# The dt product of the first queries: a score buffer as its target instead of the projections' bank

## The chip, the cores and the metric

The kernel runs on one core of a Trainium2 chip. The metric is the time of one execution on the device in microseconds (us). TensorE is called PE here, ScalarE ACT, VectorE DVE, GpSimd POOL and SyncE SP; PSUM is the memory of eight banks into which PE writes its products.

## The reference, cut to what matters

Two layers over 1024 latent tokens and 256 context tokens of width 1024: attention first, then a Mamba-2 style scan (SSD). Each layer norms its input, shifts and scales it, and adds its gated result back.

```python
h, hc = x, ctx
for i in range(DEPTH):                      # DEPTH = 2
    u = rms_normalize(h) * (1.0 + scale[:, None]) + shift[:, None]
    uc = rms_normalize(hc) * (1.0 + scale_c) + shift_c
    if i % N_MIXERS == 0:
        y, yc = attention_mixer(u, uc, ...)
    else:
        y, yc = ssd_mixer(u, uc, ...)
    h = h + gate[:, None] * y
    ...
# in ssd_mixer, for the context and for the latent tokens
z, xbc, dt_raw = jnp.split(h @ w_in, [SSD_WIDTH, SSD_WIDTH + SSD_CONV_DIM], axis=-1)
xbc = silu(centred_depthwise_conv(xbc, conv_w, conv_b))
dt = softplus(dt_raw.reshape(...) + dt_bias_dir)
```

`dt_raw` is a product of the normed input with 64 columns of the input weights. From `dt` come the decays of the scan, which all heads need.

## The kernel before, in words

Tokens are held in three blocks: block 0 (latent 0 to 511), block 1 (latent 512 to 1023) and block 2 (the 256 context tokens). The normed and modulated input of each block stands in two parts, `uH` and `uL`, a rounded value and its rest, and so does each weight (`wh`, `wl`); a product is three matmuls for each of the eight slices of the width (lines 238 to 240, in `mm3`).

Attention's PSUM holds two score buffers `S` of two banks each, one bank `pj` for projections, two `pt` and one `pv`. A call of `t(pool, ...)` takes the next buffer of its name, and the first instruction that writes it waits until the last reader of its former content is done.

At the end of `attention` the last block (block 1) has its output product made for eight column groups, m = 0 to 7; those with m % 3 other than 0 use a score buffer, the others `pj`. Each is read by a gate on DVE (line 840), squared on ACT (847) and summed on DVE (848, `sqa`). Then `dt_setup` has loaded the weights of dt (`wdth`, `wdtl`), and a loop makes two dt products, of block 2 (256 columns) and of block 0 (512 columns), each read by four ACT instructions in `dt_raw` (line 1013, into `cacc`). Last comes `steps[-1]()`: the norm of block 1 and its modulation. The norm sums the squares across partitions on PE (line 361, into `pt`), takes the root on ACT and POOL (369, 370), spreads it by a diagonal (DVE 376, PE 378), and copies the result on ACT (380); the modulation writes `uH1` and `uL1` (299 to 301).

Behind it the scan's layer opens other PSUM pools (`psD`, `psX`, `pj2`) in the same banks. `front` makes the input products of group 0, tile by tile: bT (which becomes B), two tiles of x, cT. For each tile there is a product of the context (line 1179, into `psD`) and one of the latent tokens (1194, into `pj2`), then taps of the convolution on ACT (1093) and DVE (1097), a silu (ACT 1108, DVE 1106), and PE transposes (1148) with ACT copies (1149). In among the first tile stands the third dt product, that of block 1 (line 1204, into `psX`), and when it is read the chain of dt begins (lines 1061 to 1081, mostly DVE), with PE transposes at 1050. Each tile's weights are cast on ACT (1123) and split on DVE (1127). The states of the scan (1297 on PE, 1309 on DVE, `hb`) follow.

The order of all this on each engine isn't written by hand alone. The program is laid out ahead of time by a scheduler with a timeline of its own, which places an instruction where, by that timeline, its engine and data are free. Each engine then works its list off in order.

Of the kernel before, what the change touches and what calls it, by code (L numbers as in the profile page):

```python
# [42 lines left out]
    pj=1, S=2, pt=2, pv=1,  # L43
# [70 lines left out]
class Kernel:  # L114
# [684 lines left out]
    def attention(self, c0, ckv):  # L799
        nc, t, a = self.nc, self.t, self.a  # L800
        ps = self.psA
# [109 lines left out]
        for x, (i, j, b) in enumerate(units):  # L911
            if oH[i] is None:
                if i == 1:
                    i = 0
                    tick(True)
                    i = 1
                    cq.close()
                    self.po = self.pool("op", ctx=c0)
                n = TT[i][1]
# [12 lines left out]
        with ExitStack() as c1:  # L932
            self.o1 = self.pool("o1", ctx=c1, side="right")
            steps = out_steps(1)
            for f in steps[:-1]:
                for _ in f():
                    pass
            self.dt_setup()
            for i, lo in ((2, 256), (0, 0)):
                n = TT[i][1] // 2  # L940
                self.dt_raw(self.dts[:, lo : lo + n], self.proj(ps, self.wdt, i), n)
            for _ in steps[-1]():
                pass
        BUFS.update(wr=2, wh=2, wl=2)
# [852 lines left out]
```

## Time and profile before

| | us |
|---|---|
| median of 3 runs (lowest, highest) | 1774.34 (1774.31, 1775.89) |
| the profiled execution | 1774.14 |
| its span, first to last instruction | 1772.0 |
| PE busy | 1726.3 (97%) |
| DVE busy | 1204.1 (68%) |
| ACT busy | 872.3 (49%) |
| POOL busy | 795.5 (45%) |
| mean granted clock of TensorE | 0.997 |

In the views, a timeline row gives the start, the duration, the engine, the line, the operation, what it writes from what it reads, the count, and in brackets how long the engine was idle before it and what ended that. Matmuls overlap: one of 512 columns has a duration of 0.39 us and follows the one before after 0.23. A row of the chain gives start, time on the chain, engine, tile and line. A row of the waits gives the sum, the count and the longest. A row of stretches gives the span, PE's busy time and instructions, the granted clock of TensorE, the DMA share and GB/s.

### The profile page before, as it was taken

The page shows a single profiled execution, that of the slowest core. Times are in us where ns is not written, and L with a number is a line of the kernel's source. Part 1 is how long each engine was busy: PE and PEld are TensorE (multiplying, and loading weights), DVE is VectorE, ACT ScalarE, POOL GpSimd, SP SyncE. Part 2 cuts the span into 40 slices and gives each one's busy share as a digit, 9 for nine tenths or more (in the row PEclk, how much of TensorE's full clock was granted, in tenths as well). Part 3 has the DMA queues.
Part 4 walks back from the last instruction along what each step waited for, and adds up shares of the span by engine and source line. Part 5 has one row for each costly group of instructions (what it writes and reads, how often), then busy time and mean ns, then how long its engine had stood idle before and what let it go on. Part 6 is the DMA issues. An engine that isn't in the chain of part 4 may idle for free.

```text
span 1772.0 us, 28996 instructions
## 1 busy us (share of the span) xinstructions
PE 1726.3 (97%) x10327; PEld 1492.7 (84%) x10327; DVE 1204.1 (68%) x2121; ACT 872.3 (49%) x1902; POOL 795.5 (45%) x1066
## 2 busy tenths in 40 slices
PE   6999999999999999999999999999999999999997
PEld 4897788888888887778898998989889898988887
DVE  5744447788877775694876867677686767866634
ACT  4522247777787774452544434344444434544522
POOL 3231037555575545104454554636355363554321
PEclk9999999999999999999999999999999999999999
DMA  9568856444464536231323232322333333556533
GB/s 356 174 204 272 294 140 149 101 102 106 115 159 125 131 105 212 72 76 56 76 79 98 72 93 69 87 78 75 90 81 83 81 84 81 183 162 168 183 100 119
DMA packets 211355, 225.51 MB, mean 127 GB/s; under 512 B 15756, under 2 KB 149004, under 8 KB 211212
## 3 DMA queue, kind: packets, MB, share of 16 engines
q1 hardware_dynamic: 177148, 205.02, 39.0%
q0 software_dynamic: 34064, 18.65, 5.7%
q8 instruction: 81, 1.33, 0.3%
q14 instruction: 62, 0.51, 0.1%
HBM read 188.78 MB, written 35.13 MB: 126 GB/s over the span
## 4 chain that ended last, share of the span: by engine, by line
PE 84%; DVE 7%; issue 3%; DMA 2%; ACT 2%; POOL 1%; SPq 0%; DVEq 0%; POOLq 0%; ACTq 0%
PE pj L1194 19%; PE pj L1228 10%; PE pj L1629 7%; PE pj L238 6%; PE pj L240 6%; PE pj L239 6%; PE psD L1179 4%; PE pt L774 3%; PE psX L1381 3%; PE psD L1297 2%; PE pv L781 2%; PE pv L780 2%; PE psX L1350 2%; PE psX L1349 2%; PE S L749 2%
## 5 line engine op out<-in xcount | busy, mean ns | idle before, releaser
L238 PE MATMUL pj<-uH,wh 128*128 128x512 f32 (+1 forms) x680 | 243.8, 359 | 1.3 <-ACT uH L796 0.4
L240 PE MATMUL pj<-uH,wl 128*128 128x512 f32 (+1 forms) x680 | 229.8, 339 | 1.4 <-POOL wl L223 1.4
L239 PE MATMUL pj<-uL,wh 128*128 128x512 f32 (+1 forms) x680 | 230.0, 338 | 0.4 <-POOL uL L797 0.4
L1194 PE MATMUL pj<-uH,wh 128*128 128x512 f32 x512 | 173.4, 410 | 1.2 <-ACT bn L1149 1.2
L1194 PE MATMUL pj<-uH,wl 128*128 128x512 f32 x512 | 170.3, 403 | 0.0
L1194 PE MATMUL pj<-uL,wh 128*128 128x512 f32 x512 | 168.3, 402 | 0.0
L1272 POOL TENSOR_TENSOR xw<-xn,dtdec 128x256 f32<-128x256 f32 x144 | 95.9, 667 | 160.0 <-PE psD L1297 76.0
L1228 PE MATMUL pj<-wh,uH 128*128 128x256 f32 x512 | 150.8, 295 | 0.0
L238 PEld LDWEIGHTS pj<-uH,wh 128*128 128x128 f32 x680 | 129.0, 190 | 25.5 <-ACT wh L221 5.6
L1228 PE MATMUL pj<-wl,uH 128*128 128x256 f32 x512 | 150.2, 293 | 0.0
L1228 PE MATMUL pj<-wh,uL 128*128 128x256 f32 x512 | 149.5, 292 | 0.0
L779 DVE TENSOR_TENSOR pl<-pt,ph 128x512 fp32r<-128x512 f32 x168 | 114.2, 688 | 48.0 <-ACT ph L778 46.8
L240 PEld LDWEIGHTS pj<-uH,wl 128*128 128x128 f32 x680 | 128.7, 190 | 17.5 <-POOL wl L223 2.3
L239 PEld LDWEIGHTS pj<-uL,wh 128*128 128x128 f32 x680 | 129.4, 190 | 10.7 <-issue 1.1
L223 POOL TENSOR_TENSOR wl<-wr,wh 128x512 fp32r<-128x512 f32 x74 | 96.8, 1310 | 87.8 <-ACT wh L221 87.0
L753 DVE CUSTOM_DVE_ANT_0 sm<-S,mask,nsink 128x640 f32<-128x640 f32 (+2 forms) x160 | 119.4, 772 | 21.2 <-PE S L749 15.6
L1413 ACT ACTIVATE uT<-psX,nw 128x128 f32<-128x128 f32 x128 | 46.6, 364 | 170.9 <-PE psX L1412 169.8
L755 ACT ACTIVATE sm<-sm,nm 128x640 f32<-128x640 f32 (+2 forms) x160 | 118.6, 743 | 15.3 <-DVE nm L753 14.7
L778 ACT CAST ph<-pt 128x512 fp32r<-128x512 f32 x168 | 97.6, 586 | 53.4 <-PE pt L774 49.1
L221 ACT CAST wh<-wr 128x512 fp32r<-128x512 f32 (+1 forms) x116 | 74.7, 648 | 82.1 <-PE pj L239 60.3
L1194 PEld LDWEIGHTS pj<-uH,wl 128*128 128x128 f32 x512 | 95.8, 188 | 19.9
L1194 PEld LDWEIGHTS pj<-uL,wh 128*128 128x128 f32 x512 | 95.3, 188 | 19.3
(354 smaller groups left out, 4918.1 us busy)
## 6 DMA issues: line engine op xcount, KB each, us to landing
wr<-w_x SPq DMA_DIRECT2D x32, 512.0 KB, 4.2
M<-acs SPq DMA_DIRECT2D x64, 256.0 KB, 5.1
bw<-acs SPq DMA_DIRECT2D x64, 256.0 KB, 5.5
wr<-w_sk SPq DMA_DIRECT2D x24, 512.0 KB, 4.1
wr<-wg SPq DMA_DIRECT2D x40, 256.0 KB, 4.8
qs<-q POOLq DMA_DIRECT2D x40, 256.0 KB, 3.9
wada<-w_ada SPq DMA_DIRECT2D x16, 512.0 KB, 6.5
wr<-wq SPq DMA_DIRECT2D x32, 256.0 KB, 3.1
```

The source lines that it names most:

```text
L223: (eng or nc.vector).tensor_tensor(l, raw, h, op=ALU.subtract)
L238: self.nc.tensor.matmul(ps, lh, rh, start=first and i == 0, stop=False)
L239: self.nc.tensor.matmul(ps, lh, rl, start=False, stop=False)
L240: self.last_mm = self.nc.tensor.matmul(ps, ll, rh, start=False, stop=last and i == n - 1)
L753: nc.vector.tensor_tensor_reduce(out=sm[:, :W], in0=Sv, in1=self.mask[:, m0 : m0 + W], scale=-SCALE, scalar=self.nsink[:, 4 * j + r : 4 * ...
L755: nc.scalar.activation(sm[:, :W], sm[:, :W], AF.Exp, bias=nm[:, r : r + 1], scale=-1.0, accum_out=sums[:, r : r + 1])
L778: nc.scalar.copy(ph, ptf)
L779: nc.vector.tensor_sub(pl, ptf, ph)
L1194: self.pe = nc.tensor.matmul(raw[:, 512 * i : 512 * i + 512], l[:, k, :], r[i][:, k, :], start=k + y == 0, stop=k == KT - 1 and y == 2)
L1228: self.pe = nc.tensor.matmul(pj[:, c], l, r[:, k, :], start=c % 2 + q + k + y == 0, stop=c % 2 == 1 and q == 1 and k == 3 and y == 2)
L1272: nc.gpsimd.tensor_tensor(xw, X(st, c).rearrange("p (r h) -> p r h", r=R), self.dtdec[:, c, hd(d, g)].unsqueeze(2).broadcast_to([P, R, HP] ...
L1629: self.pe = nc.tensor.matmul(banks[x], l[:, z, sl], r, start=k == 2 * qs[0] and y == 0, stop=k == 2 * qs[-1] + 1 and y == 2)
```

## The change

The product of block 0 is written into a score buffer (`psS`, two buffers of two banks) and no more into `pj`. The product of block 2 stays in `pj`. No product, reading or transfer is added or dropped.

```diff
             for i, lo in ((2, 256), (0, 0)):
                 n = TT[i][1] // 2
-                self.dt_raw(self.dts[:, lo : lo + n], self.proj(ps, self.wdt, i), n)
+                self.dt_raw(self.dts[:, lo : lo + n], self.proj(ps, self.wdt, i, "pj" if i else "S"), n)
```

The scheduler's timeline comes out differently from this place on, until the first slots of the scan, and with it the order on PE, ACT, DVE and (one row) POOL. SP's list stays as it was.

On PE, at the end of attention: `S_8569` is the last output group, `pj_8612` the dt product of block 2, number 8641 that of block 0, `pt_8670` the norm's sum and `pt_8680` its spreading.

```order
 L239 MATMUL S_8569<-uL_1372_5690,wh_8557 128x512
+L238 MATMUL S_8641<-uH_2036_8183,wdth_8601 128x512
 L240 MATMUL S_8569<-uH_1371_5689,wl_8559 128x512
...
 L240 MATMUL pj_8612<-uH_1656_6760,wdtl_8603 128x256
+L239 MATMUL S_8641<-uL_2037_8184,wdth_8601 128x512
...
 L361 MATMUL pt_8670<-ones_68,sqa_8289 128x1 x4
-L238 MATMUL pj_8641<-uH_2036_8183,wdth_8601 128x512
...
 L378 MATMUL pt_8680<-dg_2131_8678,ones_68 128x512
```

The product of block 0 moved ahead of the norm's sum, one of its 24 matmuls into the last output group, and the sum and its spreading now follow each other. Further on PE, eight matmuls of line 1194 that stood ahead of the end of the third dt product (1204) stand behind it; the two transposes (1148) of the first x tile's context product follow directly on the eight of bT; and the eight transposes of that x tile stand behind 24 matmuls of line 1194 and nine of line 1179.

On ACT, at the same place (`rc` is the norm's root, `wh_8833` the cast of the third dt product's weights):

```order
 L1013 ACTIVATE cacc_8611<-pj_8612,db_8605 32x128 x4
+L1123 CAST wh_8833<-wr_8783 128x1024
+L1013 ACTIVATE cacc_8611<-S_8641,db_8605 32x256 x4
 L369 ACTIVATE rc_8675<-pt_8670,eps_70 128x4
-L1123 CAST wh_8833<-wr_8783 128x1024
-L1013 ACTIVATE cacc_8611<-pj_8641,db_8605 32x256 x4
 L380 COPY sqa_8682<-pt_8680 128x512
```

The reading of block 0's product moved ahead of the norm's first step.

On DVE, in the first tiles of the scan's layer: before, from the reciprocal of the dt chain on (`cctx_9009` and `cacc_8926` belong to the first x tile, `wl_9116` is the second x tile's weight).

```order
L1066 RECIPROCAL sz_8885<-sz_8884 128x640
L1106 SCALAR_TENSOR_TENSOR bT_8812<-pj_2172_8811,bT_8812 128x1024
L1097 SCALAR_TENSOR_TENSOR cctx_9009<-psD_8964,cw_8735,cctx_9009 128x254
L1067 TENSOR_TENSOR xn_2178_8883<-xn_2178_8883,sz_8885 128x640
L1127 TENSOR_TENSOR wl_9116<-wr_9061,wh_9114 128x1024
```

And now, the last twelve rows up to the silu of that context product:

```order
L1069 SCALAR_TENSOR_TENSOR cacc_8611<-cacc_8611,xn_2178_8883 128x640
L1097 SCALAR_TENSOR_TENSOR cctx_9009<-psD_8964,cw_8735,cctx_9009 128x255
L1127 TENSOR_TENSOR wl_9116<-wr_9061,wh_9114 128x1024
L1097 SCALAR_TENSOR_TENSOR cacc_8926<-pj_2187_8925,cw_8735,cacc_8926 128x1022
L1070 TENSOR_SCALAR sz_8884<-cacc_8611 128x640
L1071 TENSOR_SCALAR xn_2178_8883<-cacc_8611,al_8607 128x640
L1097 SCALAR_TENSOR_TENSOR cctx_9009<-psD_8964,cw_8735,cctx_9009 128x254
L1106 SCALAR_TENSOR_TENSOR bT_8812<-pj_2172_8811,bT_8812 128x1024
L1097 SCALAR_TENSOR_TENSOR cacc_8926<-pj_2187_8925,cw_8735,cacc_8926 128x1023
L1072 SCALAR_TENSOR_TENSOR sz_8885<-cT_8767,xn_2178_8883 64x640
L1073 SCALAR_TENSOR_TENSOR sz_8885<-cT_8767,xn_2178_8883 64x640
L1106 SCALAR_TENSOR_TENSOR cctx_9009<-psD_8964,cctx_9009 128x256
```

The end of bT's silu (the row L1106 of bT) stood directly behind the reciprocal; now the dt steps 1067 to 1071, the four taps of cctx, the split of the next weight and a tap of cacc stand between them. Two dt steps (1063, 1064) moved the other way, ahead of the split that opens this stretch.

## The prediction

> **What bounds the kernel now.** I read the page's head and its chain first, then who waited for whom on TensorE (PE) between 700 and 870 us, the stretch in which attention hands over to the scan, then the timelines of each engine there, and last the chain in order of time.
>
> ```profile
> span 1772.0 us, 28996 instructions
> PE 84%; DVE 7%; issue 3%; DMA 2%; ACT 2%; POOL 1%; SPq 0%; DVEq 0%; POOLq 0%; ACTq 0%
> ```
>
> PE carries 84% of the chain that ended last. The rows of PE's timeline follow its program's order, with no gap over most of the span, so a microsecond that PE waits is a microsecond of the end, unless a later PE wait becomes shorter by it. The profiled execution took 1774.14 us, its span 1772.0; the median of the three runs is 1774.34, 0.2 above it.
>
> Two waits concern the changed product directly: PE's timeline shows both, each for the reading of the one bank `pj` by ScalarE (ACT).
>
> ```profile
> 719.30 0.28 PE L238 MATMUL pj<-uH,wdth 128*128 128x256 f32 x1
> 722.10 0.95 PE L361 MATMUL pt<-ones,sqa 128*128 128x1 f32 x8
> 724.16 0.50 PE L238 MATMUL pj<-uH,wdth 128*128 128x512 f32 x1 [1.11 <-ACT cacc L1013]
> 729.85 1.02 PE L378 MATMUL pt<-dg,ones 128*128 128x512 f32 x2
> 732.00 0.38 PE L1179 MATMUL psD<-uH,wh 128*128 128x256 f32 x1 [1.13 <-ACT cacc L1013]
> ```
>
> The context's dt product ends at 722.10; the first queries' product may begin only when ACT has emptied the bank (1.11 us lost); the scan's first product (L1179) waits for the second emptying (1.13 lost). Between them stand the norm's sum (L361) and, behind the second product, its spreading (L378), for which nothing was waited.
>
> **The change part by part.** *The two waits (removed).* With a score buffer as its target the second product needs no emptying of `pj`, and the scan's first product finds `pj` read long before. That is 1.11 + 1.13 = 2.24 us of PE waits. Against that, one matmul of the product is now placed inside the last output block's product, where it needs the score buffer's last reader, the gate of block 5:
>
> ```profile
> 713.53 0.74 DVE L840 SCALAR_TENSOR_TENSOR h1k<-S,mod,h1k 128x512 f32<-128x512 f32 x1
> 714.04 0.39 PE L239 MATMUL S<-uL,wh 128*128 128x512 f32 x1
> ```
>
> That reader ends at 714.27, the moment at which PE gets there (714.04 plus one spacing of 0.23). I take 0.1 us, between 0 and 0.3.
>
> *The norm's chain (a new wait).* L361 now stands behind the second product instead of ahead of it, and on ACT the first step of the norm (L369) stands behind the reading of the score buffer. L378 follows L361 directly on PE, so nothing covers the chain in between any more. Its steps:
>
> ```profile
> 722.63 1.47 ACT L1013 ACTIVATE cacc<-pj,db 32x128 f32<-32x128 f32 x4
> 724.13 0.26 ACT L369 ACTIVATE rc<-pt,eps 128x4 f32<-128x4 f32 x1
> 730.05 1.90 ACT L1013 ACTIVATE cacc<-pj,db 32x256 f32<-32x256 f32 x4 [4.72 <-PE pj L240]
> 724.48 1.02 POOL L370 TENSOR_TENSOR rc<-rc,half 128x4 f32<-128x4 f32 x1 [7.41 <-ACT rc L369]
> 726.50 0.68 DVE L376 TENSOR_TENSOR dg<-ident,rc 128x512 f32<-128x512 f32 x1
> ```
>
> PE: 719.30 + 0.23 (the early matmul) + 0.1 + 2.80 (the context's product, 722.10 - 719.30) = 722.4; 23 matmuls of 0.23 (5.7 us from 724.16 to 729.85 for 24) bring 727.8; the last one's tail, 0.39 - 0.23, gives 727.95. Then 1.90 (L1013) + 0.26 (L369) + 0.1 lag + 1.02 (GpSimd) + 0.05 + 0.68 (VectorE) = 4.0: L378 begins near 732.0 and L1179 some 0.85 later, at 732.85, where it was 732.00. PE idles 3.4 us between L361 and L378. So this place alone ends **0.85 us later**, the 2.24 included.
>
> *The order on VectorE (moved, and the largest term).* The order is made ahead of time by a scheduler, and behind the handover it comes out otherwise. On VectorE (DVE) the taps of bT (L1097, L1106) are now mixed with the dt chain and with the next tile's taps, and PE's transposes of bT (L1148) still stand where they stood.
>
> ```profile
> 750.21 1.91 ACT L1013 ACTIVATE cacc<-psX,db 32x256 f32<-32x256 f32 x4
> 752.13 1.06 ACT L1123 CAST wh<-wr 128x1024 fp32r<-128x1024 f32 x1
> 754.58 0.75 ACT L1062 ACTIVATE xn<-xn 128x640 f32<-128x640 f32 x1
> 752.14 0.82 DVE L1061 SCALAR_TENSOR_TENSOR xn<-cacc 128x640 f32<-128x640 f32 x1 [0.58 <-ACT cacc L1013]
> 753.22 1.23 DVE L1127 TENSOR_TENSOR wl<-wr,wh 128x1024 fp32r<-128x1024 f32 x1 [0.25 <-ACT wh L1123]
> 766.04 1.09 PE L1148 MATMUL pj<-ident,bT 128*128 128x128 f32 x8 [0.52 <-DVE bT L1106]
> 768.30 0.74 PE L1194 MATMUL pj<-uH,wh 128*128 128x512 f32 x2 [1.16 <-ACT bn L1149]
> ```
>
> Before, PE reaches the transposes at 765.5 and waits 0.52 us for L1106 of bT; 1.16 us more for the copy behind them. After, PE reaches them 0.85 later, at 766.4. For DVE: the third dt product (L1204) has eight L1194 matmuls fewer ahead of it (8 x 0.23 = 1.8), so ACT's reading of it ends 1.8 - 0.85 = 0.95 earlier, at 751.15; L1061 (0.82), L1062 (0.75) and only then the cast L1123 (1.06) bring 753.8, and the split L1127 begins at 753.85, 0.6 later than its 753.22. Two dt steps (L1063, L1064, 0.40 each) are now done ahead of it. These steps come in between it and L1106 of bT, by the chain's rows:
>
> ```profile
> 757.33 0.40 DVE sz L1064
> 766.37 0.73 DVE xn L1067
> 767.11 1.13 DVE wl L1127
> 768.24 0.39 DVE cctx L1097
> 768.63 1.19 DVE cacc L1097
> 772.14 0.73 DVE cacc L1069
> 774.45 0.40 DVE sz L1070
> 774.85 0.46 DVE xn L1071
> 775.32 0.33 DVE cctx L1106
> 776.84 1.39 DVE sz L1072
> 778.26 1.50 DVE sz L1073
> ```
>
> L1067, L1068 and L1069 at 0.73 each, four taps of cctx at 0.39, the split L1127 1.13, one tap of cacc 1.19, L1070 0.40, L1071 0.46: 6.93 us. L1106 of bT ends 0.6 - 0.80 + 6.93 = 6.7 us later, at 772.75. PE waits 6.35 us there instead of 0.52.
>
> *The next transposes.* Those of the context tile (cctx) now follow at once on PE. Their data come after one tap of cacc, L1072, L1073 and L1106 of cctx: 1.19 + 1.39 + 1.50 + 0.33 = 4.4 us behind L1106 of bT, at 777.15, while PE ends the eight transposes at 773.85: 3.3 us idle. With 0.2 for the two transposes PE begins L1194 of the next tile at 777.35 where it began at 768.30: 9.05 later, of which 0.2 is work done ahead.
>
> *What gets shorter behind that.*
>
> ```profile
> PE pj L1148 <- DVE cacc L1106: 1.4, 1, 1.4
> PE psD L1297 <- DVE hb L1309: 1.2, 2, 0.6
> ...
> 831.86 0.45 PE psD L1297 x2
> 832.88 0.71 PE psD L1297 x2
> ```
>
> Late PE work finds DVE further on: the wait of 1.4 for cacc goes (those transposes now stand behind 33 matmuls, 24 x 0.23 + 9 x 0.12 = 6.6 us, and DVE needs two taps, L1106 and some small dt steps, about 5 us). The state products (L1297) move forward by one place each, so that the bunch at the end, where a pair takes 0.71 instead of 0.45 and the waits sum to 1.2, shrinks: between 1.2 and 2.5 us, I take 2.0. Sum without the clock: 9.05 - 0.2 - 1.4 - 2.0 = **5.45 us**.
>
> *The clock.* The only idle stretch of over 1.4 us in this trace that has work behind it stands at the start:
>
> ```profile
> 24.13 0.80 PE L516 MATMUL pj<-uH,wh 128*128 128x512 f32 x1 [2.79 <-ACT uH L540]
> ...
> 22.00:26.00 4.00, 1.87 (x4) 0.72 1.05 402
> 26.00:30.00 4.00, 4.00 (x24) 0.85 0.90 345
> ```
>
> The granted clock (third figure from the right) falls to 0.72 and 0.85 in those two stretches of 4 us: 4 x 0.28 + 4 x 0.15 = 1.7 us of PE's work lost once, behind an idle time of 2.79. Idle times of 1.1 to 1.4 us show no such loss. The new ones, 3.4, 6.35 and 3.3 us, are all longer; the last two lie a microsecond apart and count as one, and the first is interrupted by L361. I take one loss of 1.6, between 0 and two of them. [...]
>
> Sum: 5.45 + 1.6 = 7.05; 1774.14 + 7.05 = 1781.2 for a profiled execution, 1781.4 beside the median.
>
> **The rivals.** *No loss of clock.* The same waits, PE at full speed behind them: 1774.34 + 5.45 = 1779.8. For it: only one place in the trace shows the loss. Within the forecast's sign. *Two losses*: the wait at L378 has one too, 1774.34 + 5.45 + 3.2 = 1783.0.
>
> *Faster: the freed bank decides.* If bT's taps do not hold PE, because DVE has the reordered steps done by the time PE comes, the handover's 2.24 us of waits, the 1.16 behind the transposes and the 1.4 for cacc are gone with the 2.0 of the state products, and the chain at L378 eats the handover's gain: 1774.34 - 1.16 - 1.4 - 2.0 + 0.85 = 1770.6. It decides if L1106 of bT ends less than 0.5 us behind PE's arrival; by the sums above it is 6.35 behind. Against it: the steps ahead of it are on one engine in a fixed order and their durations are measured. Only a misread order could turn it.
>
> *No difference.* PE loses at the handover but the scan gives most of it back, since its other waits shrink as well. From the list of waits between 700 and 870 us no more than the 1.2 to 2.5 us already counted is there to be given back in this stretch, and later stages of the chain are PE end to end. It would take 3.5 us more than that: 1779.8 - 3.5 = 1776.3.
>
> *The change does nothing there*, if the score buffer shares the wait: the product's 1.11 would stay. It has another reader, gone by 714.27.
>
> **How the numbers follow.** A measurement of this kernel can tell some 0.2%, 3.5 us, from no change: slower is above 1777.9, faster below 1770.8. The forecast with one loss of clock has 0.5, none 0.2, two 0.15: together 0.85, all slower. No difference 0.09, faster 0.06. Bounds: with no loss and 2.5 us given back, 5.45 - 0.5 = 4.95 us, 1779.3; two losses and only 1.2 given back, 5.45 + 0.8 + 3.2 = 9.45 us, 1783.8. I widen the low end by 1.3 for the four durations on DVE that other work could shorten, and leave out the two cases of 0.15: 1778.0 to 1784.0.
>
> **What would show it.** In the profile after: no wait of L238 and L1179 for L1013; a PE wait of 3 to 4 us at L378 for the norm's diagonal (L376); 6 to 7 us at L1148 for L1106 of bT; 3 to 4 us at the transposes of cctx; none at L1148 for L1106 of cacc; granted clock below 1 in one or two stretches near 770 to 785; every stage behind 870 us equally long, only later by 5 to 9. It is wrong if PE's wait for bT is below 3 us, if DVE's steps from that split L1127 to L1106 of bT take much less than 19 us (753.85 to 772.75), or if the shift at 870 us is gone by the end.

## The result, and the profile after

The changed kernel takes 1784.57 us (median of six runs), the kernel before beside it 1775.12: **slower by the ratio 1.0056 (95% interval 1.0039 to 1.0074)**, some 9.9 us. In a second comparison it was 1784.32 to 1775.02, ratio 1.0054 (1.0041 to 1.0066). The forecast was 1781.4 in a range of 1778.0 to 1784.0: the direction held, the size was 3 us short, just past the range's upper end.

The list of waits of TensorE (PE) in the changed kernel, 700 to 885 us (total, times, longest):

```profile
PE pj L1148 <- DVE bT L1106: 6.2, 1, 6.2
PE pt L378 <- DVE dg L376: 3.4, 1, 3.4
PE psD L1148 <- DVE cctx L1106: 2.6, 1, 2.6
```

That is all of it: both waits for the reading of `pj` (L1013) are gone, and so are those for `bn`, `cacc` and `hb`. Three long ones stand in their place. PE's timeline at the three, and the first rows behind:

```profile
729.36 0.95 PE L361 MATMUL pt<-ones,sqa 128*128 128x1 f32 x8
733.72 2.04 PE L378 MATMUL pt<-dg,ones 128*128 128x512 f32 x2 [3.41 <-DVE dg L376]
...
775.85 1.97 PE L1148 MATMUL pj<-ident,bT 128*128 128x128 f32 x8 [6.21 <-DVE bT L1106]
780.41 0.69 PE L1148 MATMUL psD<-ident,cctx 128*128 128x128 f32 x2 [2.59 <-DVE cctx L1106]
780.75 1.20 PE L1194 MATMUL pj<-uH,wh 128*128 128x512 f32 x2
```

Behind each wait the work itself is slow: L378 takes 2.04 us where it took 1.02, bT's eight transposes 1.97 where they took 1.09. The view of stretches says why. The stretches here are cut at the moments where the granted clock changes (span, PE busy, instructions, granted clock, DMA share, GB/s):

```profile
733.63:737.05 3.42, 3.33 (x9) 0.50 0.02 5
...
771.18:774.59 3.41, 0.00 (x0) 1.00 0.37 108
774.59:778.00 3.41, 1.97 (x8) 0.50 0.11 46
778.00:781.42 3.42, 1.01 (x4) 0.50 0.07 18
781.42:784.83 3.41, 3.41 (x10) 0.50 0.24 69
784.83:788.24 3.41, 3.41 (x17) 1.00 0.65 94
```

The clock is at half for one piece of 3.41 us behind the wait at L378, and for three such pieces around the two sets of transposes. What that costs: 3.33 us of PE work at half speed lose 1.67 us; bT's transposes lose nothing, since they end 2.59 us ahead of the next ones' data; from 780.41 to 784.83 PE works at half speed and loses 4.42 / 2 = 2.21. Together **3.9 us**, where the forecast had 1.6.

The profiled execution took 1784.48 us, 10.3 more than that of before. Not all of it belongs to the change: the clock was also low for a moment ahead of the changed place, 0.83 in this stretch of 10 us, where the profile of before has 1.00.

```profile
690.00:700.00 10.00, 8.49 (x29) 0.83 0.55 175
```

Two matmuls that both kernels make give the change's share. One is the first of the context's dt product, at 719.30 in the profile of before (the prediction shows its row). The other stands behind the changed part; here it is in the profile of before, and then both in that of the changed kernel.

```profile
850.54 0.48 PE L1194 MATMUL pj<-uH,wh 128*128 128x512 f32 x1
```

```profile
721.20 0.28 PE L238 MATMUL pj<-uH,wdth 128*128 128x256 f32 x1
...
861.36 0.48 PE L1194 MATMUL pj<-uH,wh 128*128 128x512 f32 x1
```

The first starts 1.9 us later than before, the second 10.8: 8.9 us arise in between. Of these, 3.9 are clock by the sum above, which leaves 5.0 for the waits and the order.

### The profile page after: what moved, and what is told of

Same layout as the page of the kernel before. It is cut to its first block, busy times and chain, and to the rows that moved or that the text cites. A ratio compares the mean times of both kernels' runs of the same rounds, so it can differ in the third digit from the quotient of the medians.

```text
span 1782.4 us, 28994 instructions
## 1 busy us (share of the span) xinstructions
PE 1731.0 (97%) x10327; PEld 1498.0 (84%) x10327; DVE 1204.7 (68%) x2121; ACT 872.7 (49%) x1902; POOL 794.8 (45%) x1066
## 4 chain that ended last, share of the span: by engine, by line
PE 58%; DVE 2%; issue 1%; POOL 0%; ACT 0%; DVEq 0%; POOLq 0%; ACTq 0%
PE pj L1194 19%; PE pj L1228 10%; PE pj L1629 7%; PE psD L1179 4%; PE psX L1381 3%; PE psD L1297 2%; PE psX L1350 2%; PE psX L1349 2%; PE psX L1356 1%; PE pj L240 1%; PE pj L238 1%; PE pj L239 1%; PE psX L1412 1%; PE psX L1347 1%; PE pj L1148 1%
```

## The experiments

In seven of these ten kernels the order was held by a table of instruction numbers for each engine, from the end of attention to the first slots of the scan, from which edges are made that bind the order alone. Three kernels have matmuls added, which shifts line numbers there by up to 15: L1163 is L1148 here, L1117 is L1106, and L281 are the added ones. Times are medians; behind each stands the ratio to the kernel before on the same chip.

| kernel | us | before | ratio (95% interval) |
|---|---|---|---|
| bank alone, order of before | 1771.74 | 1775.29 | 0.9980 (0.9971 to 0.9989) |
| scan's order alone | 1779.17 | 1775.29 | 1.0019 (1.0010 to 1.0029) |
| handover's order alone | 1777.83 | 1775.29 | 1.0018 (1.0009 to 1.0027) |
| changed kernel, stretches filled | 1780.57 | 1775.29 | 1.0026 (1.0016 to 1.0037) |
| sum first | 1772.34 | 1775.21 | 0.9982 (0.9973 to 0.9991) |
| context's product in the score buffer | 1785.55 | 1775.21 | 1.0056 (1.0043 to 1.0069) |
| handover's order, filled | 1776.17 | 1775.21 | 1.0007 (0.9999 to 1.0016) |
| changed kernel, last stretch filled | 1781.73 | 1775.21 | 1.0032 (1.0020 to 1.0044) |
| silu's product early | 1788.56 | 1775.02 | 1.0071 (1.0058 to 1.0085) |
| changed kernel again | 1784.32 | 1775.02 | 1.0054 (1.0041 to 1.0066) |

**The bank alone.** The new bank, with every engine's order as before.

```diff
+def keep_order(tc):
+    at = {i.name: i for i in tc.nc.cur_bb.bb.instructions}
+    for row in ORDER.values():
+        row = [n for n in row if f"I-{n}" in at]
+        for x, y in zip(row, row[1:]):
...
     k.build()
+    keep_order(tc)
```

> The score buffer as the dt product's target, with every instruction on PE, DVE, ACT and POOL in the order of the kernel before. Theory (the changed order costs, the bank itself gains): both waits for L1013 (1.11 and 1.13 us) go, no wait of 3.4 us at L378 and none of 6 us at L1148 appears, no drop of the granted clock between 730 and 790 us; the kernel ends 1.5 to 2.8 us ahead of the kernel before, near 1772.9. Rival (the bank itself costs, by a reader or a transfer that the list of waits doesn't show): most of the 9.9 us stays, at least 5 us slower than before.

It is 3.6 us faster than before (0.0020 of 1775; the interval gives 2.0 to 5.1), a little more than the theory's 1.5 to 2.8, which the interval overlaps. Its waits between 700 and 885 us, without a small one behind them, are those of before less the two for L1013:

```profile
PE pj L1148 <- DVE cacc L1106: 1.4, 1, 1.4
PE psD L1297 <- DVE hb L1309: 1.2, 2, 0.6
PE pj L1194 <- ACT bn L1149: 1.2, 1, 1.2
PE pj L1148 <- DVE bT L1106: 0.5, 1, 0.5
```

So the edit that the diff shows is a gain. What loses is the order that the scheduler makes around it.

**The scan's order alone, and the handover's order alone.** The same edit with another table: up to the norm's spreading (L378) one kernel's order, behind it the other's. Against the table of the bank alone, a piece of DVE's row for the scan's order (8950 is L1106 of bT), and of PE's for the handover's (8642 is the dt product's matmul that slipped into the last output block):

```diff
-8943, 8919, 8950, 9012, 8933, 9117, 9013, 9067, 8940, 9014, 9068, 8947
+8943, 8947, 9014, 9117, 9067, 8954, 8960, 9015, 8950, 9068, 8971, 8991
```

```diff
-8571, 8572, 8573, 8574, 8575
+8571, 8642, 8572, 8573, 8574
```

> The score buffer as target; PE up to the norm's spreading (L378) and ACT up to its copy (L380) in the order of the kernel before, all behind that in the order of the changed kernel. Theory: no wait of 3.4 us at L378 and no drop of the clock there; the wait for bT at L1148 (6.2) and the one for cctx (2.6) stay, with a clock at half for some 10 us around them, of which 2 to 2.5 us cost time: 4 to 5.5 us slower than before, near 1779.5. Rival (the two places aren't independent: the lateness from the handover makes the scan's order costly): the wait for bT shrinks below 4 us, and the kernel is within 2 us of the kernel before.

> The score buffer as target; the handover (PE up to L378, ACT up to L380) in the order of the changed kernel, all behind that in the order of the kernel before. Theory: the wait of 3.4 us at L378 stays, one window of 3.4 us at half clock stands behind it, the waits at L1148 are those of before (0.5 and 1.4): waits 1 us and clock 1.5 us, 2 to 3.5 us slower than before, near 1777.7. Rival (no loss of clock behind 3.4 us of idle time; the stretch at half clock that the changed kernel shows there was chance): 0.5 to 1.2 us slower than before.

The scan's order alone: 3.4 us slower than before by the ratio (3.9 by the medians), just under what was expected, with the waits of 6.3 and 2.6. Its clock:

```profile
769.64:773.05 3.41, 1.97 (x8) 0.50 0.16 65
773.05:776.47 3.42, 1.12 (x4) 0.50 0.07 19
776.47:779.88 3.41, 3.41 (x9) 0.50 0.31 81
779.88:783.29 3.41, 3.41 (x16) 1.00 0.38 88
```

The handover's order alone: 3.2 us slower (2.5 by the medians). The wait of 3.4 us at L378 shows in the first row, one piece of half clock behind it in the second:

```profile
730.28:733.69 3.41, 0.23 (x1) 1.00 0.23 95
733.69:737.10 3.41, 3.41 (x12) 0.50 0.02 5
```

Both rivals fall, and the two places add. Against the bank alone (-3.6) the scan's order costs 3.4 + 3.6 = 7.0, the handover's 3.2 + 3.6 = 6.8, together 13.8; the changed kernel stands 9.8 + 3.6 = 13.4 above it. Each of these differences is known to some 2 us.

**The clock by itself.** The changed kernel's order, with matmuls that nobody reads in the three idle stretches.

```diff
+    def warm(self, pool, tag, size, n):
+        if n:
+            out = pool.tile([P, size], F32, tag=tag, name=f"warm_{tag}_{n}", bufs=BUFS.get(tag, 1))
+            for _ in range(n):
+                self.nc.tensor.matmul(out[:, :512], self.uH[0][:, 0, :P], self.uH[0][:, 0, :], start=True, stop=True)
...
+        if self.warming == 1:
+            self.warm(self.psS, "S", 1024, 14)
...
+                if g == 0 and d is st["bn"][0]:
+                    self.warm(ps, "psX", 512, 27)
+                if g == 0 and d is st["xn"][2] and o == 0:
+                    self.warm(ps, "psX", 512, 12)
```

> The changed kernel in its own order, with matmuls of 128x512 whose product nobody reads put on PE into its three idle stretches: 14 ahead of L378, 27 ahead of the transposes of bT, 12 ahead of those of cctx, 0.23 us each. They take no time that PE would not have waited. Theory (part of the time is TensorE's clock, which drops behind the idle stretches): the granted clock stays at 1 between 730 and 790 us, and the kernel ends 3 to 4 us ahead of the changed kernel, 5.5 to 7 us behind the kernel before, near 1781. Rival (the drops of the clock lie beside waits and cost nothing; the waits and something else make up the 9.9 us): same time as the changed kernel, 9 to 10.5 us behind the kernel before, near 1784.5.

PE's timeline (the added matmuls and the work behind them), then the stretches:

```profile
728.81 3.43 PE L281 MATMUL warm_S<-uH 128*128 128x512 f32 x14
732.36 1.10 PE L387 MATMUL pt<-dg,ones 128*128 128x512 f32 x2
...
766.55 6.28 PE L281 MATMUL warm_psX<-uH 128*128 128x512 f32 x27
772.92 1.09 PE L1163 MATMUL pj<-ident,bT 128*128 128x128 f32 x8
```

```profile
730.00:740.00 10.00, 9.88 (x53) 1.00 0.03 11
760.00:776.00 16.00, 15.91 (x80) 1.00 0.12 33
776.00:786.00 10.00, 9.31 (x55) 1.00 0.34 72
```

More work, and less time: 1780.57, 3.9 us ahead of the changed kernel by the medians (1784.4 as the mean of its two), 5.1 by the ratios (1.0055 less 1.0026). The order on DVE, ACT and POOL is that of the changed kernel, and on PE it differs by the 53 added matmuls alone. The two matmuls of above stand at 719.84 and 856.36 us in this profile: 5.3 us arise between them, 3.6 fewer than in the changed kernel's. What differs is that the clock stays up: the mean granted clock of this kernel's seven executions is 0.994 to 0.998, that of the changed kernel's eleven 0.988 to 0.994, that of the kernel before 0.992 to 0.997. So the rival falls: those 3.6 to 5.1 us are the clock (the ratios' difference is known to some 2.6 us), and the trace's own sum was 3.9.

**The handover's order, filled.** The 14 matmuls ahead of L378 alone, in the kernel with the handover's order.

```diff
+        if self.warming == 1:
+            self.warm(self.psS, "S", 1024, 14)
```

> The kernel with the handover's order alone (handover of the changed kernel, the rest as before), with 14 matmuls of 128x512 that nobody reads in the 3.4 us ahead of L378. Theory (the clock's drop behind that idle stretch cost about 1.5 us there): no drop at 733 us, 0.5 to 1.5 us slower than before, near 1776.3, and 1 to 2.5 us ahead of the same kernel without them. Rival (the drop costs nothing since the work behind it waits anyway): the same time as without them, 2.5 us slower than before.

```profile
730.00:740.00 10.00, 9.88 (x58) 1.00 0.19 65
```

No drop there, and 1776.17: 1.0 us behind the kernel before (1.2 by the ratio), 1.7 by the medians ahead of the same kernel without the fill (2.0 by the ratios, whose intervals overlap). The forecast's 0.85 for this place without the clock agrees with what is left, which the interval puts between -0.2 and 2.8.

**Only the last stretch filled.** The kernel with all three filled, with two numbers changed.

```diff
                 if g == 0 and d is st["bn"][0]:
-                    self.warm(ps, "psX", 512, 27)
+                    self.warm(ps, "psX", 512, 0)
                 if g == 0 and d is st["xn"][2] and o == 0:
-                    self.warm(ps, "psX", 512, 12)
+                    self.warm(ps, "psX", 512, 5)
```

> The changed kernel in its own order, filled ahead of L378 (14 matmuls) and, of the two later stretches, only in the last: 5 matmuls, which at half speed take 2.3 of its 2.6 us; the 6.2 us ahead of the transposes of bT stay idle. Theory (the clock comes back after one window of 3.4 us in which PE is busy; in the changed kernel the second stretch kept it low): half clock for two windows (6.8 us) instead of three, full again some 3 us earlier, 0.3 to 1 us slower than the kernel with all three filled, near 1781.2. Rival (one long idle stretch brings a fixed 10.2 us of half clock, whatever PE does behind it): half clock for 10.2 us, 2 to 2.5 us slower than the kernel with all three filled, near 1782.8.

```profile
764.92:768.33 3.41, 0.94 (x5) 1.00 0.00 0
768.33:771.74 3.41, 0.00 (x0) 0.50 0.58 154
771.74:775.16 3.42, 3.09 (x12) 0.50 0.00 0
775.16:778.57 3.41, 2.55 (x13) 1.00 0.11 29
```

Two pieces at half clock, no third: the clock is full one piece earlier, at the end of the first in which PE was mostly busy (3.09 of 3.42). The fixed 10.2 us of the rival fall by this. In the second profile of the changed kernel, shown further down, the half clock starts with a piece without work too, and lasts four pieces. The time (1.2 us behind the kernel with all three filled) lies between the two expectations and can't tell them apart, as the intervals overlap.

**One edge.** In the changed kernel block 0's product had slipped ahead of the norm's sum, its first matmul into the last output block. Here the scheduler is told to keep that first matmul behind the sum.

```diff
+                traced = nc.cur_bb.bb.instructions
+                mark = len(traced)
                 self.dt_raw(self.dts[:, lo : lo + n], self.proj(ps, self.wdt, i, "pj" if i else "S"), n)
+            first = next(x for x in traced[mark:] if x.engine == self.last_mm.ins.engine)
             for _ in steps[-1]():
                 pass
+            self.tc.add_manual_dep(first, self.sum_mm.ins.name, mybir.DependencyInfo(mybir.DependencyClass.NoSync, mybir.DependencyReason.DATA), reason="sum first")
```

> The changed kernel with one more edge for the scheduler: the first matmul of block 0's dt product may not stand ahead of the norm's sum (L361) on PE. The scheduler then lays out DVE and POOL as in the kernel before, ACT but for two swaps of neighbours, and PE but for a few rows of the first tile. Theory (one instruction that slipped ahead of the sum drew the order of all that follows): no wait for L1013, none of 3.4 us at L378, none of 6 us at L1148; 2 to 3.5 us ahead of the kernel before, near 1772.5, and 12 to 13.5 ahead of the changed kernel. Rival (the order of the scan's first tiles goes back only in part): a wait of over 3 us for bT or cctx stays, 1776 or more.

It is 3.2 us ahead of the kernel before and 12 ahead of the changed kernel. Behind that one edge the order on DVE and POOL is that of the kernel before again, on ACT but for two swaps of neighbours, on PE but for some two dozen matmuls. The wait for bT is 0.5 again; that of 1.4 for `cacc` is gone, and one of 1.1 that the kernel before hasn't stands at L1183 (L1152 there is L1148, 1110 is 1106, L1183 is L1179):

```profile
...
PE psD L1183 <- ACT xn L1153: 1.1, 1, 1.1
PE pj L1152 <- DVE bT L1110: 0.5, 1, 0.5
```

With the bank alone it shares the best time: both beat both kernels, and their intervals overlap.

**The other product in the score buffer.**

```diff
-                self.dt_raw(self.dts[:, lo : lo + n], self.proj(ps, self.wdt, i, "pj" if i else "S"), n)
+                self.dt_raw(self.dts[:, lo : lo + n], self.proj(ps, self.wdt, i, "S" if i else "pj"), n)
```

> The buffers of the two dt products exchanged against the changed kernel: that of block 2 into the score buffer, that of block 0 into pj. The scheduler's order comes out otherwise here too: one matmul of block 2's product inside the last output block, the norm's sum behind block 0's product, and another order in the scan's first tiles. Theory (the order decides, not which product has the score buffer): waits at L378 and at L1148 as in the changed kernel and idle stretches with drops of the clock, 9 to 14 us slower than before. Rival (block 0's product in the score buffer is what costs): within 3 us of the kernel before.

1785.55, 9.9 us slower than before, with the same waits of 6.2, 3.4 and 2.6. Another bank choice, the same order from the scan on, the same loss.

**One row on VectorE.** The changed kernel, with one number of DVE's table moved seven places: L1106 of bT (8950) directly behind bT's last tap (8943).

```diff
-8943, 8947, 9014, 9117, 9067, 8954, 8960, 9015, 8950, 9068
+8943, 8950, 8947, 9014, 9117, 9067, 8954, 8960, 9015, 9068
```

> The changed kernel in its own order but for one row: on DVE the silu's product of bT (L1106) stands directly behind the last tap of bT instead of seven rows later. Theory as the prediction put it (the DVE steps standing ahead of L1106 hold TensorE's transposes): the wait for bT shrinks from 6.2 us to about 2, the wait for cctx grows by as much, and the time stays within 1.5 us of the changed kernel. Rival (ACT's order holds it as well: the sigmoid that L1106 reads, L1108 of bT, ends only at 773.8 us in the changed kernel, 0.8 us ahead of L1106): DVE stands still for over 3 us in front of L1106, the wait for bT shrinks by less than 1 us, the steps of the next tile come later, and the kernel is 2.5 to 4.5 us slower than the changed kernel.

The rival holds. DVE's timeline, and PE's waits:

```profile
772.72 1.22 DVE L1106 SCALAR_TENSOR_TENSOR bT<-pj,bT 128x1024 f32<-128x1024 f32 x1 [3.83 <-ACT pj L1108]
```

```profile
PE psD L1148 <- DVE cctx L1106: 7.3, 1, 7.3
PE pj L1148 <- DVE bT L1106: 5.4, 1, 5.4
```

DVE stands still for 3.83 us in front of L1106, since ACT's sigmoid isn't ready. The wait for bT shrinks by 0.8, that for cctx grows by 4.7, and the kernel is 4.2 us slower than the changed one (3.0 by the ratios, whose intervals overlap).

**The changed kernel again.**

> The changed kernel itself once more, as the measure for the run beside it and for the kernels with filled stretches. Both theories: 9 to 10.5 us slower than before; the idle stretches of 3.4, 6.2 and 2.6 us again, each with a drop of the granted clock behind it; how many windows of 3.4 us the drop takes may differ from the first profile, if the windows run freely.

Its waits are the same three. Its clock isn't: two pieces at half at the wait for L378, four around the transposes.

```profile
733.36:736.77 3.41, 1.40 (x3) 0.50 0.02 5
736.77:740.19 3.42, 3.42 (x15) 0.50 0.00 0
...
774.32:777.73 3.41, 0.00 (x0) 0.50 0.53 154
777.73:781.15 3.42, 1.97 (x8) 0.50 0.00 0
781.15:784.56 3.41, 1.86 (x6) 0.50 0.10 27
784.56:787.97 3.41, 3.41 (x10) 0.50 0.39 96
```

This execution took 1787.78 us, that of the first profile 1784.48, with the same program and the same waits; between the two matmuls of above (722.84 and 864.05 here) 10.0 us arise, 1.1 more than in the first. Where the pieces fall against the idle time differs between the two profiles: of the first piece at half clock at L378, PE was idle for 0.09 us in the first and for 2.01 here; the kernel's five runs here lie between 1781.5 and 1787.8.

## Why the prediction was right or wrong

- **The removed waits: right.** No wait for L1013 is left, and the bank alone gains 3.6 us (2.0 to 5.1) against the 2.24 of the sum.
- **The norm's chain: right.** A wait of 3.41 us against 3.4; with the clock kept up, the handover's order ends 1.0 later (-0.2 to 2.8) against 0.85.
- **VectorE's order: the size right, the cause half right.** The transposes of bT wait 6.2 us (forecast 6.35), those of cctx 2.6 (3.3). But the forecast laid the first to the steps ahead of L1106 on DVE alone. In the changed kernel ACT's sigmoid of bT ends only 0.8 us ahead of L1106:

```profile
772.73 1.03 ACT L1108 ACTIVATE pj<-bT 128x1024 f32<-128x1024 f32 x1
```

```profile
768.69 1.27 DVE L1097 SCALAR_TENSOR_TENSOR bT<-pj,cw,bT 128x1022 f32<-128x1022 f32 x1
...
774.58 1.22 DVE L1106 SCALAR_TENSOR_TENSOR bT<-pj,bT 128x1024 f32<-128x1024 f32 x1
```

  Three of bT's four taps now stand behind the dt chain's reciprocal (4.14 us), ahead of which all four stood before. So the last tap of bT itself ends at 769.96, 9 us later than before; a cast, a tap of the next tile and a table load (1.05, 1.20 and 1.28 us, from 769.27 on) then stand on ACT ahead of the sigmoid. With the DVE row moved, only those 0.8 us came back. The orders of two engines hold the transposes, almost equally. What a change of ACT's order would bring no run shows.
- **What is given back: right.** The waits for `bn`, `cacc` and `hb` are gone. The sum without the clock was 5.45; the filled kernel, in which the clock stays up, measures 4.6 (2.8 to 6.6), and 5.3 between the two matmuls of its profile.
- **The clock: the step that failed.** "I take one loss of 1.6, between 0 and two of them" put one price, that of the start, on the whole; the stretch at L378 was dismissed as "interrupted by L361", though L361 stands ahead of it and interrupts nothing. Measured: a loss behind the wait at L378 (1.67) and one behind the transposes (2.21), 3.9 in the trace, 3.6 to 5.1 by the filled kernel. With 3.9 for 1.6 the same sum gives 5.45 + 3.9 = 9.35, 1783.7; the medians differ by 9.45. The price of the second isn't that of the start: the clock stayed at half behind the pieces with the two transposes' work (1.97 and 1.01 us of 3.41); with five more matmuls ahead of the second (3.09 us of work in a piece) it came back. The forecast didn't ask what the pieces in between would do.
- **The range.** Its upper end counted two losses of 1.6 and so stood at 1784; the runs of the changed kernel go up to 1790.4.
- **The rivals.** "Two losses" (1783.0) was nearest. "Faster: the freed bank decides" (1770.6) is near the times with the order kept, 1771.7 and 1772.3, but by another way, so its nearness is luck: it counted on the waits for `bn` and `hb` to go, which stay there (1.2 each), and what is gained are the two waits for L1013.

## What to carry to other kernels

Read a change of a buffer for what it does to the order of every engine before its own waits are priced: here the edit gains 3.6 us, the order that came with it costs 13.4, and one edge on one instruction keeps the first without the second. Here the waits of PE cost themselves and then the clock: 1.67 us more after the wait of 3.41, 2.21 more after those of 6.21 and 2.59. Each is half of the time that PE was busy at half clock behind the last wait, up to the end of a piece with 3.33 and with 3.41 us of work in it. To price another wait that way is an estimate from these two places; the last section has pieces that don't follow it. Where a wait can't go, matmuls that nobody reads kept the clock up here (3.9 us by the medians for 53 of them); they were counted so as to end about when the wait does.

## What the runs showed of the hardware that was not expected

- In the profile of before and the first of the changed kernel the granted clock of PE reads 1.00 or 0.50, and each stretch at 0.50 that ends in the span lasts one piece of 3.41 us or three: 23.76 to 27.17 in that of before; 16.83 to 27.07, 692.68 to 696.09, 733.63 to 737.05 and 774.59 to 784.83 in that of the changed kernel. In its second profile, at the rows shown above, it is two pieces (733.36 to 740.19) and four (774.32 to 787.97). At the changed place the clock came back after pieces in which PE was busy for 3.09 us (last stretch filled), 3.33 and 3.41 (changed kernel), and not after pieces of 2.49 and 2.51. In the profile of the kernel with the context's product in the score buffer:

```profile
730.57:733.98 3.41, 2.51 (x6) 0.50 0.02 7
733.98:737.39 3.41, 3.41 (x18) 0.50 0.00 0
```

  The busy time alone doesn't decide it. At the start of the changed kernel's profile a piece with 3.34 us of work (16.83 to 20.24 us, some of it eight matmuls of two columns at L399) is followed by two more at half clock; at the start of that of before a piece with 3.04 (23.76 to 27.17 us) is followed by the full clock.

- A drop also came behind a piece that was more than half busy. In the kernel with the handover's order alone, one with 2.12 us of work in it was followed by a drop; the profile of before has a piece at the same work, with as much in it, that was not.

```profile
836.09:839.50 3.41, 2.12 (x8) 1.00 0.00 0
839.50:842.91 3.41, 3.41 (x13) 0.50 0.00 0
```

```profile
832.72:836.13 3.41, 2.12 (x8) 1.00 0.00 0
836.13:839.54 3.41, 3.41 (x29) 1.00 0.10 27
```

  In the kernel with the handover's order filled, a piece with 1.74 us of work (769.34 to 772.75 us) was followed by a drop too. So a drop came behind 1.3 us of idle time in a piece (3.41 less 2.12), against the forecast's reading that idle times of 1.1 to 1.4 show no loss; what decides was not settled.

- At the start of the profile of before the granted clock doesn't tell how long a matmul takes: eight matmuls of L389 take 1.93 us at 16.31, and sixteen of the same form 1.92 at 27.57, half as long each; it reads 1.00 in both stretches.
